# A decoder step on one core: the feed-forward's weight sums move from DRAM to VectorE, gate/up takes both token halves from one weight load, down becomes a stage of its own

## The chip, the core and the metric

The kernel runs on one core of a Trainium2 chip. TensorE (PE) multiplies matrices, VectorE (DVE) and ScalarE (ACT) do elementwise work, GpSimd (POOL) does some too, and SyncE (SP) issues DMAs between DRAM and the on-chip memory SBUF. Each engine works through its own queue in order. Matrix products land in PSUM, eight banks that PE writes and DVE and ACT read. The metric is the device time of one launch in microseconds (us), smaller is better.

## What is computed

One layer of a hybrid decoder for 1024 prompt tokens and 64 sample tokens (1088 columns in all): a combined input projection, sliding-window attention and an mLSTM side by side, an output projection, cross-attention to a memory, and a SwiGLU feed-forward. All of it is float32. The part that the change rewrites is the feed-forward:

```
def swiglu(xn, w_gate, w_up, w_down):
    g = jnp.einsum('btd,df->btf', xn, w_gate)        # D_MODEL 1024 -> FFN_HIDDEN 2816
    u = jnp.einsum('btd,df->btf', xn, w_up)
    return jnp.einsum('btf,fd->btd', jax.nn.silu(g) * u, w_down)
y = y + swiglu(rmsnorm(y, g_ffn), w_gate, w_up, w_down)
y_out = rmsnorm(y, g_final)
```

## The kernel before

Every float32 product is made of three products of halves of the numbers: each operand is split into a rounded part `hi` (an ACT copy to the type fp32r) and the rest `lo` (a DVE subtraction), and `mm3` (L145) adds hi·hi, hi·lo and lo·hi in PSUM. The split of a weight tile is in `prep` (L1111): ACT L1119 and DVE L1120.

The feed-forward uses a seven-product form of the 2x2 block product (Winograd's), with blocks of 128 x 128 weights and 128 x 272 activations. It needs sums and differences of weight blocks and of activation blocks. The 1088 columns are two halves z of 544, each of two blocks of 272. The hidden width is 11 pairs p of 256. A pair of one half takes 14 products in `gate_up` (7 for gate, 7 for up, 12 matmuls each) and 7 in `down` (12 matmuls each).

- The **weight sums** are made before the feed-forward, in DRAM: `make_sums` (L179) issues 36 copies on the ACT queue (L192) into `sgu` and `sdn` and 36 accumulating DMAs on the POOL queue (L187, `accum_op=ALU.add`), one pair of them at each `next(presum)` in the attention part. The feed-forward then loads finished sums.
- The **activation sums** are made in SBUF: of the normed input in `ffn_x` (L1130), of the hidden blocks h in `parts_of` (L1070), with two differences on POOL (L1072, L1073), two more on DVE (L1079, L1080) and splits on ACT and DVE (L1083, L1084).
- The **order**: for each half, `plan` runs gate/up of three pairs, then down of two (L1101), and so on, so that gate/up and down alternate; then the other half. Weights are loaded once for each half, in tiles of 128 x 1024 (512 KB), three raw tiles and three split ones in turn. `down` adds its products from PSUM to y in SBUF on DVE (L1237). At the end `Final` sums squares (L1286, L1287) and writes the normed output (L1300).
- A scheduler orders each engine's queue from its own cost estimates when the kernel is built. A DMA waits in its queue like any instruction.

The attention part (the first 642 us) has, beside PE's work, chains that go through small DMAs: rows of the mLSTM gates are written to DRAM and read back broadcast (`bc` from Md, `wb` from Wd and Wds), masks are loaded (`msk`), y is loaded (L797), weights of the projections (`wraw`, L120).

Of the kernel before, what the change touches and what calls it, by code (L numbers as in the profile page):

```python
# [44 lines left out]
def tile_hymba_step(  # L45
# [118 lines left out]
    sgu = dr.tile([NP2, P, 8, 512], F32, name="sgu")  # L164
    sdn = dr.tile([NP2, P, 4, 512], F32, name="sdn")

    def sums_of(a, b, gu):
        def v(t, i, step):
            t = t[a:b].rearrange("n p e c -> (n p) e c")
            return t[:, i:i + step + 1:step] if gu else t[:, i]  # L170
        if gu:
            R11, R12, R22, R21 = v(wgu, 0, 2), v(wgu, 1, 2), v(wgu, 4, 1), v(wgu, 6, 1)
            s2, s1, s3, s4 = v(sgu, 0, 2), v(sgu, 1, 2), v(sgu, 4, 2), v(sgu, 5, 2)
        else:
            R11, R12, R22, R21 = v(wdn, 0, 1), v(wdn, 1, 1), v(wdn, 2, 1), v(wdn, 3, 1)
            s2, s1, s3, s4 = v(sdn, 0, 1), v(sdn, 1, 1), v(sdn, 2, 1), v(sdn, 3, 1)
        return (s1, R21, R22), (s3, R11, R21), (s2, R11, s1), (s4, R12, s2)

    def make_sums():  # L179

        parts = ([sums_of(a, min(a + 2, NP2), True) for a in range(0, NP2, 2)]
                 + [sums_of(a, min(a + 4, NP2), False) for a in range(0, NP2, 4)])
        copied = []

        def add():
            dst, plus = copied.pop(0)
            tc.keep_in_program_order(G.dma_start(dst, plus, accum_op=ALU.add))  # L187

        for i in range(4):
            for part in parts:  # L190
                dst, src, plus = part[i]
                tc.keep_in_program_order(A.dma_start(dst, src))  # L192
                if len(copied) == 3:
                    add()
                copied.append((dst, plus))
                yield
        while copied:
            add()
            yield
# [107 lines left out]
    for b in range(NB + 1):  # L307
        acc, m = tok_gemm(wb, b, 384)
        r = rt[:m, b:b + 1]
        A.activation(mvx[b // 2][:m, b % 2, 1:4, 0:P],  # L310
                     acc[:m, 0:384].rearrange("p (h e) -> p h e", h=3), AF.Copy, scale=r)
        if b % 3 == 2:
            next(presum)
# [177 lines left out]
    for i, (wi_, pre) in ((1, (2, 0.125)), (2, (3, None)), (3, (4, None))):  # L491
# [9 lines left out]
        next(presum)  # L501
# [123 lines left out]
    for blk in range(NB):  # L625
        if blk == 4:
            mlstm_sample()
            next(presum)
# [23 lines left out]
        next(presum)  # L652
# [383 lines left out]
    sg = slot("r", [4, HC], name="sg")  # L1036

    def ffn_rstd(ci, s_ps):

        mm(s_ps, ones, sg[:, ci])  # L1040
        return rstd_from(rf[:, ci * HC:ci * HC + HC], s_ps, D)

    for ci, (c0, c1) in enumerate(CX):
        ss = sg[:, ci]
        for d in range(NK):
# [24 lines left out]
    def parts_of(out, S):  # L1070

        G.tensor_tensor(S[:, N1], S[:, B11], S[:, B12], ALU.subtract)  # L1072
        G.tensor_tensor(S[:, T3], S[:, B22], S[:, B12], ALU.subtract)  # L1073
        parts(out, S, 4, 7)
        sums_of_blocks(S)
        parts(out, S, 0, 4)

    def sums_of_blocks(S):
        V.scalar_tensor_tensor(S[:, N2], S[:, N1], -1.0, S[:, B22], ALU.mult, ALU.subtract)  # L1079
        V.scalar_tensor_tensor(S[:, T4], S[:, N2], -1.0, S[:, B21], ALU.mult, ALU.subtract)  # L1080

# [12 lines left out]
    def dn_tiles(ps_):
        for src, i in ((wdn, 0), (sdn, 0), (sdn, 2)):
            for p in ps_:
                yield [src[p, :, i:i + 2, :]]
        for i in range(0, len(ps_), 2):
            yield [wdn[p, :, 2:3, :] for p in ps_[i:i + 2]]

    plan = [("gu", 0)]  # L1101
    for g0 in range(0, NP2 - 1, 2):
        plan += [("gu", g0 + 1), ("gu", g0 + 2), ("dn", list(range(g0, g0 + (3 if g0 == 8 else 2))))]

    def tiles_of(plan):
# [3 lines left out]
    todo, ahead = iter([t for _ in range(2) for t in tiles_of(plan)]), []

    def prep():  # L1111
        for srcs in todo:
            raw = fp.tile([P, 2, 512], F32, tag="wr", name="wr", bufs=3)
            i = 0
            for a in srcs:
                nc.sync.dma_start(raw[:, i:i + a.shape[1]], a)
                i += a.shape[1]
# [10 lines left out]
    prep()  # L1128

    def ffn_x(z):  # L1130

        xo, xs = [], []
        for j in range(4):
            S = fp.tile([P, 8, HC], F32, tag="ho" if z == 0 and j > 1 else "hs", name="xs",
                        bufs=3 if z == 0 and j > 1 else 2)
            for i, d in ((B11, j), (B21, j + 4)):
                V.scalar_tensor_tensor(S[:, i:i + 2].rearrange("p a c -> p (a c)"), y[d][:, z * SET:z * SET + SET],  # L1137
                                       gcol(V_FFN, d), rf[:, z * SET:z * SET + SET], ALU.mult, ALU.mult)
            t = fp.tile([P, 2, 7, HC], F32R, tag="xo", name="xo", bufs=4)
            xo.append(t)  # L1140
            if z > 0:
                parts_of(t, S)
                continue
            parts(t, S, 4, 7)
            xs.append(S)
        for S in xs:
            G.tensor_tensor(S[:, N1], S[:, B11], S[:, B12], ALU.subtract)
            G.tensor_tensor(S[:, T3], S[:, B22], S[:, B12], ALU.subtract)
        for S, t in zip(xs, xo):
            sums_of_blocks(S)  # L1150
            parts(t, S, 0, 4)
# [308 lines left out]
```

## Time and profile before

| | |
|---|---|
| time, median of 3 runs (lowest to highest) | 1392.54 us (1391.67 to 1392.87) |
| the profiled execution: its own time, its span | 1396.1 us, 1394.3 us |
| PE matmul busy | 1291.6 us, 93% |
| DVE busy | 938.5 us, 67% |
| ACT busy | 684.2 us, 49% |
| POOL busy | 211.2 us, 15% |
| DMA moved | 244.12 MB |

The span runs from the first to the last instruction. A row of a timeline has its start and duration in us; an idle time of the engine before it stands at the end in brackets, with what ended it ("<-"). `xN` merges N instructions. In a row of stretches, (xN) counts instructions, and PEclk is the TensorE clock granted, 1.00 being the upper of its two levels (2.4 GHz) and 0.50 the lower (1.2 GHz). An instruction of DVE may start before the one ahead of it has ended, so that N of a kind take less than N times their duration.

### The profile page before, as it was taken

To read this page: it belongs to the slowest core of one execution; us is meant where nothing else is said; L and a number is where in the kernel's file an instruction comes from. 1 tells how busy PE (TensorE), PEld (TensorE's weight loads), DVE (VectorE), ACT (ScalarE), POOL (GpSimd) and SP (SyncE) were. 2 spreads that over 40 slices of the span, in tenths; PEclk is the share of its full clock that TensorE was granted. 3 is DMA by queue.
4 is the path that set the end of the run, shared out by engine and by line. 5 is a ranking of instruction groups with operands and counts; after the bars stand their busy time and mean duration, and the time that the engine had idled before them with its cause. 6 is when DMAs were issued, how large, how long until landed. Compare 5 with 4: busy or idle time off the path is not lost.

```text
span 1394.3 us, 23826 instructions
## 1 busy us (share of the span) xinstructions
PE 1291.6 (93%) x9194; PEld 1204.0 (86%) x9194; DVE 938.5 (67%) x1854; ACT 684.2 (49%) x1332; POOL 211.2 (15%) x182
## 2 busy tenths in 40 slices
PE   6999987989989969997999999999998999999996
PEld 6999976877767868765999999999997999999995
DVE  7224333436665656878777878787988868687777
ACT  4332332334755445655654554545567454545463
POOL 2000120220111365314010100001210000101010
PEclk9999988997989999997899999999999999999998
DMA  5167594793999899421555565555455555555543
GB/s 224 38 199 193 156 209 125 198 232 88 243 300 265 232 280 196 137 76 46 162 174 178 156 193 164 180 167 176 154 167 188 180 182 172 177 174 174 175 158 117
DMA packets 96330, 244.12 MB, mean 175 GB/s; under 512 B 10081, under 2 KB 17697, under 8 KB 96217
## 3 DMA queue, kind: packets, MB, share of 16 engines
q1 hardware_dynamic: 61273, 173.40, 39.2%
q0 software_dynamic: 17472, 34.61, 14.7%
q10 hardware_dynamic: 17472, 34.61, 7.3%
q8 instruction: 72, 1.18, 0.3%
q14 instruction: 41, 0.34, 0.1%
HBM read 235.19 MB, written 76.59 MB: 224 GB/s over the span
## 4 chain that ended last, share of the span: by engine, by line
PE 34%; DVE 12%; issue 3%; ACT 3%; POOL 1%; POOLq 0%; DVEq 0%; ACTq 0%
PE b L90 34%; DVE wo L1120 4%; ACT wo L1119 2%; DVE ho L1084 2%; DVE y L1237 1%; POOL h L1072 1%; DVE xo L1084 1%; DVE yo L1300 1%; DVE h L1172 1%; DVE xs L1137 1%; ACT kp L1176 0%; DVE h L1212 0%; DVE h L1204 0%; DVE sg L1201 0%; DVE h L1201 0%
## 5 line engine op out<-in xcount | busy, mean ns | idle before, releaser
L90 PE MATMUL b<-xo,wo 128*128 128x272 f32 x3696 | 476.1, 291 | 17.1 <-ACT wo L1119 7.2
L90 PEld LDWEIGHTS b<-xo,wo 128*128 128x128 f32 x3696 | 470.1, 191 | 22.3 <-ACT wo L1119 8.2
L1120 DVE TENSOR_TENSOR wo<-wr,wo 128x1024 fp32r<-128x1024 f32 x232 | 282.2, 1223 | 104.4 <-ACT wo L1119 104.1
L1119 ACT ACTIVATE wo<-wr 128x1024 fp32r<-128x1024 f32 x232 | 244.0, 1053 | 194.0 <-PE b L90 135.3
L90 PE MATMUL b<-ho,wo 128*128 128x272 f32 x1848 | 237.4, 289 | 5.0 <-DVE wo L1120 2.7
L90 PEld LDWEIGHTS b<-ho,wo 128*128 128x128 f32 x1848 | 233.2, 188 | 8.0 <-DVE wo L1120 4.7
L1072 POOL TENSOR_TENSOR h<-h 128x272 f32<-128x272 f32 x22 | 35.5, 1613 | 587.3 <-DVE h L1172 568.4
L90 PE MATMUL mm<-xhi,whi 128*128 128x384 f32 (+1 forms) x288 | 100.6, 349 | 5.9 <-DVE og L785 5.9
L1237 DVE TENSOR_TENSOR y<-y,b 128x272 f32<-128x272 f32 x280 | 103.0, 429 | 4.3 <-PE b L90 4.1
L90 PE MATMUL mm<-xhi,wlo 128*128 128x384 f32 (+1 forms) x288 | 99.5, 345 | 0.0
L90 PE MATMUL mm<-xlo,whi 128*128 128x384 f32 (+1 forms) x288 | 99.3, 345 | 0.0
L1176 ACT ACTIVATE kp<-b 128x272 f32<-128x272 f32 x132 | 51.5, 394 | 62.9 <-PE b L90 61.9
L108 ACT ACTIVATE whi<-wraw 128x1024 fp32r<-128x1024 f32 x39 | 41.0, 1054 | 70.1 <-PE mm L90 49.8
L90 PE MATMUL mm<-chi,wlo 128*128 128x384 f32 (+1 forms) x192 | 66.6, 348 | 3.7 <-POOL wlo L109 3.6
L90 PE MATMUL mm<-chi,whi 128*128 128x384 f32 (+1 forms) x192 | 67.5, 354 | 2.2 <-ACT whi L108 1.7
L90 PE MATMUL mm<-clo,whi 128*128 128x384 f32 (+1 forms) x192 | 66.4, 346 | 0.0
L90 PEld LDWEIGHTS mm<-xhi,whi 128*128 128x128 f32 x288 | 56.7, 197 | 9.5 <-DVE og L785 6.2
L90 PEld LDWEIGHTS mm<-xlo,whi 128*128 128x128 f32 x288 | 56.6, 197 | 3.1 <-issue 2.0
L90 PEld LDWEIGHTS mm<-xhi,wlo 128*128 128x128 f32 x288 | 56.4, 196 | 3.2 <-issue 1.9
L1084 DVE TENSOR_TENSOR ho<-h,ho 128x816 fp32r<-128x816 f32 (+1 forms) x44 | 48.6, 1141 | 0.0
L1083 ACT ACTIVATE ho<-h 128x816 fp32r<-128x816 f32 (+1 forms) x44 | 42.0, 994 | 11.8 <-DVE h L1212 9.9
L1169 ACT ACTIVATE sg<-sg 128x272 f32<-128x272 f32 x66 | 27.9, 423 | 40.3 <-DVE sg L1201 33.2
(369 smaller groups left out, 1983.9 us busy)
## 6 DMA issues: line engine op xcount, KB each, us to landing
wr<-sgu SPq DMA_DIRECT2D x88, 512.0 KB
wr<-wgu SPq DMA_DIRECT2D x66, 512.0 KB
wr<-sdn SPq DMA_DIRECT2D x44, 512.0 KB
sgu<-wgu ACTq DMA_DIRECT2D x20, 1024.0 KB
wr<-wdn SPq DMA_DIRECT2D x22, 512.0 KB
sgu<-wgu POOLq DMA_DIRECT2D x10, 1024.0 KB, 13.1
sgu<-sgu POOLq DMA_DIRECT2D x10, 1024.0 KB, 20.0
sdn<-wdn ACTq DMA_DIRECT2D x8, 1024.0 KB
```

Of the source, the lines that this page charges most:

```text
L90: return TE.matmul(out, lhsT, rhs, start=start, stop=stop, skip_group_check=skip)
L108: A.activation(hi, src, AF.Copy)
L1072: G.tensor_tensor(S[:, N1], S[:, B11], S[:, B12], ALU.subtract)
L1083: A.activation(out[:, 0, i:j], S[:, i:j], AF.Copy)
L1084: V.tensor_tensor(out[:, 1, i:j], S[:, i:j], out[:, 0, i:j].bitcast(F32), ALU.subtract)
L1119: A.activation(w[:, 0, :i], raw[:, :i], AF.Copy)
L1120: V.tensor_tensor(w[:, 1, :i], raw[:, :i], w[:, 0, :i].bitcast(F32), ALU.subtract)
L1137: V.scalar_tensor_tensor(S[:, i:i + 2].rearrange("p a c -> p (a c)"), y[d][:, z * SET:z * SET + SET], gcol(V_FFN, d), rf[:, z * SET:z * SE ...
L1169: A.activation(sg[:, i], sg[:, i], AF.Silu, scale=scale)
L1172: V.scalar_tensor_tensor(t, t, scale, sg[:, i], ALU.mult, ALU.mult)
L1176: A.activation(t, src, AF.Copy)
L1237: V.tensor_tensor(y[d][:, c0:c0 + HC], y[d][:, c0:c0 + HC], src[dp], op)
```

## The change

It drops `make_sums` with its 72 DMAs and the DRAM tile `sgu`. The feed-forward becomes two stages.

In **gate/up** each weight block (128 x 512, 256 KB) is loaded raw, and `sums` makes the four sums of it in SBUF. For 7 of the 11 pairs both halves z use each split weight tile in turn, so that loads, sums and splits are made once for both; the first two and the last two pairs are done for one half at a time ("single units"), there two of the four sums are on POOL. Of the 15 units, each splits 14 tiles. The results h go to DRAM (`hd`). While a pair is at half 1, `dn_sums` also makes the four sums of its down weights on DVE and stores them (`sdn`). y is put aside in DRAM (`yd`).

**Down** runs after all of gate/up: six groups (4, 4, 3 pairs for each half). h is read back in `h_parts`, which makes all four differences on POOL and splits on ACT and DVE for the next group while a group runs.

```diff
-        for i in range(4):
-            for part in parts:
-                dst, src, plus = part[i]
-                tc.keep_in_program_order(A.dma_start(dst, src))
-                if len(copied) == 3:
-                    add()          # G.dma_start(dst, plus, accum_op=ALU.add)
...
-        next(presum)
...
-    def parts_of(out, S):
-        G.tensor_tensor(S[:, N1], S[:, B11], S[:, B12], ALU.subtract)
-        G.tensor_tensor(S[:, T3], S[:, B22], S[:, B12], ALU.subtract)
...
+    def parts(out, i, src):
+        n = src.shape[1]
+        A.activation(out[:, 0, i:i + n], src, AF.Copy)
+        V.tensor_tensor(out[:, 1, i:i + n], src, out[:, 0, i:i + n].bitcast(F32), ALU.subtract)
+    def diffs(b11, b12, b21, b22, n1, m2, t3, t4, e1=G, e2=G):
+        e1.tensor_tensor(n1, b11, b12, ALU.subtract)
+        e1.tensor_tensor(t3, b22, b12, ALU.subtract)
+        e2.tensor_tensor(m2, n1, b22, ALU.add)
+        e2.tensor_tensor(t4, m2, b21, ALU.subtract)
...
+    def sums(r11, r12, r21, r22, e=V):
+        e.tensor_tensor(s1, r21, r22, ALU.add)
+        V.scalar_tensor_tensor(m2, s1, -1.0, r11, ALU.mult, ALU.subtract)
+        e.tensor_tensor(s3, r11, r21, ALU.add)
+        V.tensor_tensor(s4, r12, m2, ALU.subtract)
...
+            yield from sums(*r, e=V if len(zs) > 1 else G)
...
+    def dn_sums(p):
+        for i, t in enumerate(sums(*[raw(wdn[p, :, i, :]) for i in range(4)])):
+            nc.sync.dma_start(sdn[p, :, i, :], t)
...
+    units = ([(p, (z,)) for z in range(2) for p in (0, 1)] + [(p, (0, 1)) for p in range(2, NP2 - 2)]
+             + [(p, (z,)) for z in range(2) for p in (NP2 - 2, NP2 - 1)])
+    downs = [(z, g) for z in range(2) for g in (range(0, 4), range(4, 8), range(8, NP2))]
...
-            w = fp.tile([P, 2, 2, 512], F32R, tag="wo", name="wo", bufs=3)
-            A.activation(w[:, 0, :i], raw[:, :i], AF.Copy)
-            V.tensor_tensor(w[:, 1, :i], raw[:, :i], w[:, 0, :i].bitcast(F32), ALU.subtract)
+            w = fp.tile([P, 2, 512], F32R, tag="wo", name="wo", bufs=5)
+            A.activation(w[:, 0], t, AF.Copy)
+            V.tensor_tensor(w[:, 1], t, w[:, 0].bitcast(F32), ALU.subtract)
...
+    def x_second(j):
+        norm(a[:, 2:4], j, 1)
+        norm(b[:, 2:4], j + 4, 1)
+        parts(t, B11, a[:, 2:3])
+        parts(t, B21, b[:, 2:4])
+        diffs(a[:, 2], a[:, 3], b[:, 2], b[:, 3], a[:, 0], a[:, 1], b[:, 0], b[:, 1])
+        parts(t, N1, a[:, 0:2])
+        parts(t, T3, b[:, 0:2])
...
+            def product(b, i, start, then):
+                w = next_w()
+                for z in zs:
+                    for j in range(4):
+                        mm3(b[z], w[:, 0, j * P:j * P + P], w[:, 1, j * P:j * P + P],
+                            xo[z][j][:, 0, i], xo[z][j][:, 1, i], start and j == 0, j == 3, True)
+                    then(z, b[z])
...
+        for z in zs:
+            nc.sync.dma_start(hd[z, p], S[z])
+    def h_parts(z, p, tag):
+        hb, hn = slot(tag, [4, HC], name="hb"), slot(tag, [4, HC], name="hn")
+        nc.sync.dma_start(hb, hd[z, p])
+        t = big("ho")
+        parts(t, B21, hb[:, 0:3])
+        diffs(hb[:, 2], hb[:, 3], hb[:, 0], hb[:, 1], hn[:, 0], hn[:, 1], hn[:, 2], hn[:, 3])
+        parts(t, N1, hn)
...
+    xo[0] = x_first()
+    for u, (p, zs) in enumerate(units):
+        gate_up(u, p, zs)
+        if u < 2:
+            xo[1] += [x_second(2 * u), x_second(2 * u + 1)]
+    load_yy(0, "z")
+    hs = [h_parts(0, p, "m") for p in downs[0][1]]
...
+    for i, (z, g) in enumerate(downs):
+        if i == 3:
+            load_yy(1, "m")
+        nz, ng = downs[i + 1] if i + 1 < len(downs) else (0, ())
+        hs = down(z, hs, [(nz, p, "m" if i < 3 else "z") for p in ng],
+                  (lambda d, cc: fin[0].add(d, cc, False)) if i == 2 else fin[1].add if i == 5 else None,
+                  first_final if i == 3 else None)
```

In the attention part POOL's queue loses its DMAs. Before, around the sample tokens of the mLSTM (QZ, bcs) and the block behind them (bc, wb):

```order
L187 DMA sdn<-wdn 512x512
L587 MEMSET QZ 128x1088
L187 DMA sdn<-wdn 512x512
L553 TENSOR_TENSOR bcs<-c,bcs 64x256
L553 TENSOR_TENSOR bc<-c,bc 128x512
L637 TENSOR_TENSOR wb<-mqk,wb 128x128 x2
L187 DMA sdn<-wdn 384x512
```

The same place in the changed kernel:

```order
L593 TENSOR_TENSOR wb<-mqk,wb 128x128 x2
L544 MEMSET QZ 128x1088
L510 TENSOR_TENSOR bcs<-c,bcs 64x256
L510 TENSOR_TENSOR bc<-c,bc 128x512
L593 TENSOR_TENSOR wb<-mqk,wb 128x128 x2
```

The DMAs of line 187 are gone, the rest keeps its order.

On DVE, where a gate/up ends and a down of two pairs begins before (wo is a split weight tile, ho a split of h, y<-y,b the adding of a product):

```order
L1120 TENSOR_TENSOR wo<-wr,wo 128x1024
L1079 SCALAR_TENSOR_TENSOR h<-h 128x272
L1212 SCALAR_TENSOR_TENSOR h<-b,sg 128x272
L1080 SCALAR_TENSOR_TENSOR h<-h 128x272
L1120 TENSOR_TENSOR wo<-wr,wo 128x1024
L1084 TENSOR_TENSOR ho<-h,ho 128x816
L1084 TENSOR_TENSOR ho<-h,ho 128x1088
L1237 TENSOR_TENSOR y<-y,b 128x272 x8
L1120 TENSOR_TENSOR wo<-wr,wo 128x1024 x2
```

And in the changed kernel, in its down stage, in the second group (hb is the h read back, hn POOL's four differences of it):

```order
L1036 TENSOR_TENSOR ho<-hb,ho 128x816
L1036 TENSOR_TENSOR ho<-hn,ho 128x1088
L1227 TENSOR_TENSOR yy<-yy,b 128x272 x4
L1095 TENSOR_TENSOR wo<-wr,wo 128x512 x3
L1036 TENSOR_TENSOR ho<-hb,ho 128x816
L1095 TENSOR_TENSOR wo<-wr,wo 128x512
L1036 TENSOR_TENSOR ho<-hn,ho 128x1088
L1227 TENSOR_TENSOR yy<-yy,b 128x272 x4
L1095 TENSOR_TENSOR wo<-wr,wo 128x512 x4
```

The two differences that DVE made (lines 1079, 1080) are POOL's now, and each stretch of four additions has one pair's splits of h beside it, where these stood between gate/up units before.

## Rows read from the trace of the kernel before

**Rows 1.** Stretches: busy us (xcount) of PE, PEld, DVE, ACT, POOL; PEclk, DMA, GB/s.

```profile
642.00:666.50 24.50, 12.60 (x45) 9.29 (x43) 24.17 (x31) 13.62 (x19) 10.56 (x9) 0.59 0.20 65
1000.00:1100.00 100.00, 92.04 (x694) 89.06 (x694) 86.89 (x141) 65.12 (x97) 11.68 (x11) 0.98 0.55 173
1200.00:1300.00 100.00, 99.33 (x792) 98.89 (x791) 80.24 (x126) 51.53 (x70) 7.27 (x6) 1.00 0.55 172
```

**Rows 2.** Timeline of PE, attention part, rows after a long idle time.

```profile
194.17 0.80 PE L90 MATMUL pt<-mvx,S 128*128 128x129 f32 x2 [5.52 <-DVE S L562]
231.18 3.67 PE L90 MATMUL pt<-CS,QZ 128*64 128x129 f32 x16 [7.00 <-DVE QZ L593]
315.10 0.63 PE L90 MATMUL mm<-xhi,whi 128*128 128x320 f32 x1 [5.89 <-DVE og L785]
414.05 0.42 PE L90 MATMUL sc<-khi,qhl 64*128 64x256 f32 x2 [3.61 <-DVE qhl L109]
436.61 1.14 PE L769 MATMUL pt<-c,sp 128*128 128x128 f32 x8 [3.33 <-DVE sp L679]
493.97 0.44 PE L90 MATMUL mm<-chi,wlo 128*128 128x384 f32 x1 [1.79 <-POOL wlo L109]
522.47 1.68 PE L90 MATMUL sc<-kvhl,qhl 64*128 64x256 f32 x12 [5.58 <-ACT qhl L108]
```

**Rows 3.** Timeline of POOL, DVE and ACT ahead of five of these.

```profile
191.33 1.26 POOL L553 TENSOR_TENSOR bc<-c,bc 128x512 f32<-128x512 f32 x1 [15.86 <-DMA bc<-Md]
230.65 1.64 DVE L593 TENSOR_TENSOR QZ<-mqk,wb 64x32 f32<-64x32 f32 x8 [8.01 <-DMA wb<-Wds]
310.82 0.36 DVE L709 CUSTOM_DVE_ANT_0 spS<-sc,msk 128x192 f32<-128x192 f32 x1 [7.86 <-DMA msk<-cst_sw]
413.24 0.56 DVE L864 TENSOR_TENSOR y<-y,mm 128x384 f32<-128x384 f32 x1 [3.75 <-DMA y<-xT]
517.60 1.06 ACT L108 ACTIVATE whi<-wraw 128x1024 fp32r<-128x1024 f32 x1 [5.80 <-DMA wraw<-wout]
```

**Rows 4.** Queues from 350 to 440 us: packets, MB, share of the 16 DMA engines.

```profile
q0 software_dynamic: 4484, 8.90, 57.5%
q10 hardware_dynamic: 5001, 9.90, 31.7%
```

**Rows 5.** Stretches of the attention part.

```profile
150.00:350.00 200.00, 179.01 (x1114) 150.67 (x1113) 88.19 (x285) 70.65 (x244) 36.19 (x40) 0.91 0.72 174
350.00:450.00 100.00, 90.19 (x587) 71.03 (x585) 60.54 (x235) 59.63 (x191) 13.24 (x11) 0.95 1.08 272
450.00:560.00 110.00, 93.71 (x547) 85.25 (x545) 67.28 (x119) 52.08 (x114) 54.02 (x35) 0.95 0.94 231
```

**Rows 6.** Timeline of DVE in the feed-forward.

```profile
796.04 2.86 DVE L1237 TENSOR_TENSOR y<-y,b 128x272 f32<-128x272 f32 x8
798.82 2.35 DVE L1120 TENSOR_TENSOR wo<-wr,wo 128x1024 fp32r<-128x1024 f32 x2
```

**Rows 7.** Groups by form on DVE: busy us, mean ns | idle before, releasers.

```profile
L1120 DVE TENSOR_TENSOR wo<-wr,wo 128x1024 fp32r<-128x1024 f32 x230 | 280.9, 1227 | 104.4 <-ACT wo L1119 104.1
L1300 DVE SCALAR_TENSOR_TENSOR yo<-y,vv,rf 128x272 f32<-128x272 f32 x32 | 13.6, 495 | 4.3 <-ACT rf L161 4.3
```

**Rows 8.** Timeline: POOL and DVE at the same time, twice.

```profile
639.62 2.48 POOL L1052 TENSOR_TENSOR sg<-sg,sq 128x272 f32<-128x272 f32 x3 [3.53 <-ACT sq L1051]
640.58 0.44 DVE L1009 TENSOR_TENSOR y<-y,mm 128x272 f32<-128x272 f32 x1 [0.30 <-PE mm L90]
...
518.73 2.35 POOL L109 TENSOR_TENSOR wlo<-wraw,whi 128x1024 fp32r<-128x1024 f32 x1 [5.16 <-ACT whi L108]
519.66 1.83 DVE L115 SCALAR_TENSOR_TENSOR nhl<-y,vv,nhl 128x384 fp32r<-128x384 f32 x1 [6.96 <-ACT nhl L114]
521.88 0.60 DVE L115 SCALAR_TENSOR_TENSOR nhl<-y,vv,nhl 128x384 fp32r<-128x384 f32 x1
```

**Rows 9.** Timeline of POOL: a difference of 512 columns.

```profile
156.16 1.30 POOL L553 TENSOR_TENSOR bc<-c,bc 128x512 f32<-128x512 f32 x1 [32.42 <-DMA bc<-Md]
```

More of the change, by code (lines that the diff above doesn't have):

```diff
@@ L1109, in tile_hymba_step, with big @@
[L1109 to L1120 removed]
+    def big(name):
+        return fp.tile([P, 2, 7, HC], F32R, tag="big", name=name, bufs=8)
@@ new lines, in tile_hymba_step, with all_ops @@
+    downs = [(z, g) for z in range(2) for g in (range(0, 4), range(4, 8), range(8, NP2))]
+    def all_ops():
+        for p, zs in units:
+            yield from gu_ops(p, zs)
+            if zs[-1] == 1:
+                dn_sums(p)
+        for z, g in downs:
+            yield from dn_ops(g)
+    todo, ahead = all_ops(), []
+    def prep():
+        for t in todo:
+            w = fp.tile([P, 2, 512], F32R, tag="wo", name="wo", bufs=5)
+            A.activation(w[:, 0], t, AF.Copy)
+            V.tensor_tensor(w[:, 1], t, w[:, 0].bitcast(F32), ALU.subtract)
@@ L1206, in gate_up @@
[L1206 to L1219 removed]
+            product(b1, T3, False, result(H22, "p5", -1.0))
@@ new lines, in gate_up @@
+            product(b3, B22, False, result(H12, "p16"))
+            product(b1, T4, False, last)
+        for z in zs:
[7 more added lines that the diff above has]
+        parts(t, N1, hn)
+        return t
@@ L1220, in down, with second, product @@
+    yy = [[None] * 4, [None] * 4]
+    def down(z, hs, ahead_of, done=None, after_first=None):
+        n, nxt, ahead_of = len(hs), [], iter(ahead_of)
         b1 = [bank(i) for i in (1, 2, 6, 7)]
-        b2 = [bank(i) for i in (4, 5, 0, 3)]
-        b3 = [None] * 4
-        def prod(b, ws, o, i, start, e):
+        def second():
+            return [bank(i) for i in (4, 5, 0, 3)]
+        def product(b, i, start, dd, cc, op=ALU.add, last=False, also=None):
             for q in range(n):
-                w, o_ = ws(q, o)
+                w = next_w()
@@ new lines, in product @@
+                        V.tensor_tensor(v, v, b[dp], op)
+                        if last and done:
+                            done(2 * dp + dd, cc)
+            for a in ahead_of:
+                nxt.append(h_parts(*a))
+                break
+        product(b1, B11, True, 0, 0)
+        if after_first:
+            after_first()
+        product(second(), B21, True, 0, 0, last=True)
+        product(b1, M2, False, 0, 1)
+        b3 = second()
+        product(b3, N1, True, 1, 1, ALU.subtract)
@@ L1272, in tile_hymba_step @@
+        product(b1, T3, False, 1, 1, ALU.subtract, last=True)
+        product(b3, B22, False, 0, 1, last=True)
+        product(b1, T4, False, 1, 0, ALU.subtract, last=True)
+        return nxt
     class Final:
@@ L1306, in tile_hymba_step @@
[L1306 to L1322 removed]
+            if self.n[cc] == NK and now:
+                self.out(cc, bank((2, 0)[cc]))
@@ new lines, in tile_hymba_step, with first_final @@
+    fin = [Final(0), Final(1)]
+    def first_final():
+        for cc in range(2):
+            fin[0].out(cc, bank((3, 0)[cc]))
+    for i, (z, g) in enumerate(downs):
[5 more added lines that the diff above has]
+                  first_final if i == 3 else None)
```

313 lines of the change are left out of this document (103 added, 210 removed).

## The prediction

> **What bounds the kernel now.** I read first how full each stretch of the feed-forward is. From 1200 to 1300 us PE is busy 99.33 of 100 us at the full clock, 792 matmuls at 0.1254 us each [rows 1]: that pace is the floor there, and the change leaves the number of matmuls (5544 in the feed-forward) and their shape alone. PE falls short of it in three places. From 642 to 666.5 us the normed input is made and DVE is busy 24.17 of 24.5 us; from 1000 to 1100 us the second half's input is made and the first half's output written, and only 694 matmuls run; and there is a short tail. In the steady stretch DVE has a fifth of its time left. Next I read PE's timeline in the attention part for long idle times, and who released them. Seven rows [rows 2] show 5.52, 7.00, 5.89, 3.61, 3.33, 1.79 (the first of three like it) and 5.58 us, some 36 us in all. Going back from each to the engine ahead of it, I find a DMA: bc from Md, wb from Wds, the masks, y from xT, projection weights [rows 3]. The DMA engines are full there: from 350 to 440 us the accumulating queue q0 and the copying queue q10 alone, which carry only the weight sums, take 57.5% and 31.7% of all sixteen [rows 4]. PE also runs part of this time at the lower clock after such gaps: mean granted 0.91, 0.95 and 0.95 over 200, 100 and 110 us [rows 5], or 18 + 5 + 5.5 = 28.5 us of work lost.
>
> **Part 1, the 72 DMAs go.** At best all 36 us of idle time and 24 of the 28.5 us of clock come back (-60). At worst nothing does, because each wait names only what came last, and a softmax or mLSTM step on DVE and ACT may be ready barely earlier (0). The small loads (a 64-row broadcast that kept DVE idle 8.01 us, masks 7.86 us [rows 3]) should lose most of their time with 89% of the traffic gone, so I take two thirds of the idle time, 24 us, and 13 us of the clock: **-37**. Next late are then the in-order chains of ACT and DVE.
>
> **Part 2, the second half's input no longer cuts the feed-forward in the middle.** The stretch from 1000 us lacks (792 - 694) x 0.1254 = 12 us against the steady one [rows 1]: **-12**. Its work returns in parts 3 and 4, counted there.
>
> **What DVE's new work costs.** Instructions behind one another overlap a little. Eight additions of 272 columns take 2.86 us and one 0.44 [rows 6, 8], so each takes (2.86 - 0.44) / 7 = 0.346 us. Two splits of 1024 take 2.35 us and one 1.23 [rows 6, 7], so 1.12. On the line through both, 512 columns take 0.59, 544 take 0.63, 816 take 0.91, 1088 take 1.19. The output multiplication, 0.495 alone [rows 7], takes 0.40 in a row. On POOL a difference of 272 takes 2.48 / 3 = 0.83 [rows 8], one of 512 takes 1.30 [rows 9].
>
> A unit of both halves has 14 splits, 8 sums of gate/up and 4 of down (26 x 0.59) and 20 evacuations of 272 (6.9): 22 us of DVE beside 336 x 0.1254 = 42 us of PE, and no POOL. All of that is hidden, against 80% of DVE before; I count 0 for the seven units.
>
> POOL and DVE are not independent. Beside three POOL sums an addition that reads y and PSUM still takes 0.44 us, but a DVE instruction with its operands in SBUF, 0.60 alone, takes 1.83 and ends with the POOL split that runs from 518.73 to 521.08 [rows 8]. So POOL's time can be added to DVE's when DVE works on SBUF operands. I call s the share of POOL's time that DVE loses. It lies between 0 and 1. In the stage of part 4 the instructions on SBUF alone are 141 of 223 us (185 less 39 of additions and 5 of evacuations from PSUM), 0.63; I take 0.6.
>
> **Part 3, the first four single units.** Until the fourth has ended DVE's queue has 16 normings of 544 (10.0 us), the splits of the input (17.3), 8 differences (2.8), 58 weight splits (34.4), 27 sums (16.0) and 40 evacuations (13.8), 94.3 us. PE needs 4 x 168 x 0.1254 = 84.3 us and starts in earnest 22 us after DVE [rows 1], as before: 106.3. POOL adds the differences of the second half's input, 16 x 0.83, and 16 sums, 16 x 1.30, 34.1 us. DVE's excess is 94.3 + 34.1 s - 106.3: at s = 0.6 **+8**, at most +22, at least 0.
>
> **Part 4, from the last two single units to the fourth group of down.** Here 131 splits (77.7), 14 sums (8.3), 20 evacuations (6.9), 20 times the two splits of h (41.8), 112 additions to y (38.8), 14 sums of squares (4.8) and 16 output multiplications (6.4) make 184.7 us on DVE. PE needs 2 x 168 + 15 x 84 matmuls: 200.1 us; five split tiles ahead, 12 matmuls each, are 7.5 us more. POOL has 8 sums (10.4) and 80 differences (66.4): 76.8 us, where before a pair had two short ones. Excess 184.7 + 76.8 s - 207.6: at s = 0.6 **+23**, from 0 to +54. Reading h back costs no more than that: 7 x 256 KB and 544 KB a pair in 84 x 0.1254 = 10.5 us are 227 GB/s, which at the 0.55 share for 172 GB/s [rows 1] fills 0.73 of the DMA engines. A wait that this adds: DVE stands at the split of hn until POOL's four differences are done, with the weight splits behind it, and PE waits for those once its five tiles are used up.
>
> **Part 5, shorter distances.** In a single unit a bank is evacuated within one product of 12 matmuls, 1.5 us. Most of the 112 evacuations (0.44 us) fit; about a third may stand behind a split and cost 0.1: **+4** (0 to 12).
>
> **Sum.** -37 - 12 + 8 + 23 + 4 = -14 on the profiled execution's 1396.1 us, 1382; the runs' median, 1392.5, lies 3.6 below that execution, so 1379. In s the sum is 111 s - 80, zero at s = 0.72.
>
> The Trainium skill ("SBUF — State Buffer", who interferes with whom) says that the port that GpSimd shares with VectorE is an exclusive lock when the VectorE instruction has two SBUF inputs, and that an instruction with one does not contend. Both rows above agree. It gives no share s; taken at its hardest, with no POOL time beside additions, the sum would be that of s = 1, which is the end of rival A.
>
> **Rivals.**
>
> - A, POOL holds DVE and DVE sets the pace of down: s from 0.72 up. For it: the four differences stand behind one another in POOL's queue, in the same stretches as the splits of h and the weight splits, and DVE is in order and cannot bring its additions forward. Against it: 39 us of additions and any idle time of DVE are free for POOL. At s = 0.9 the sum is +20: 1412; at s = 1, +31: 1424. Slower. Chance 0.27.
> - B, the attention part hardly gains, because the softmax chains are late anyway. For it: before 436.61 and 414.05 PE waits on DVE itself [rows 2]. Against it: DVE's own wait ahead of that is for y's DMA, 3.75 us [rows 3]. With -8 in place of -37: +15, 1407. Chance 0.12.
> - C, nearly all of the waits and clock come back (-55) and POOL falls beside the additions and idle time (s = 0.3, parts 3 and 4 at 0): -55 - 12 + 4 = -63, 1330. Chance 0.15.
> - That the weights are still read twice for four pairs is so by the code, but changes no sum: loads are not late there now.
>
> **How the numbers follow.** The forecast, 1379, has 0.46, with 1360 to 1392 as its own range, some of it no change. A measurement of this kernel tells about 0.2% (2.8 us) from no change. Faster: the larger part of the forecast (0.40) and C (0.15), 0.55. Same: 0.08, from the edge of the forecast, A and B. Slower: the rest of A and B, 0.37. The range for 8 in 10 takes half of C and all of A but its end: 1342 to 1422.
>
> **What would show it.** In the attention part the idle rows before QZ (7.00), og (5.89) and S (5.52) shrink below 2 us and PE reaches the feed-forward near 605 us in place of 642. In the double units PE is busy 99% with DVE near 55%. In down, splits of 512 columns show a mean near 0.8 to 1 us in place of 0.69 (on the line from 0.44 to 1.23), and PE waits for wo; the matmuls of a group of three take more than 31.5 us. I am wrong if PE is 99% busy through down (C), if it stands at 85% or less there (A), or if it still waits for the DMA-fed chains before 600 us (B).

## The result and the profile after

The changed kernel takes 1404.18 us (median of 4 runs, 1403.87 to 1407.81) beside 1392.11 us (4 runs) of the kernel before: 1.0099 times the time, interval 1.0073 to 1.0124. It is slower by 12 us where 13 us faster were forecast. Its profiled execution takes 1407.81 us, its span is 1406.0 us.

The attention part gained more than forecast and the feed-forward lost more than that. The feed-forward's first product starts at 592.32 us in place of 650.33. The answer to [rows 5] in the changed kernel, the same stretches of the attention part (time, PE busy, PEld, DVE, ACT, POOL, then PE's clock, DMA share and GB/s):

```profile
150.00:350.00 200.00, 196.20 (x1283) 163.03 (x1282) 106.03 (x366) 88.41 (x305) 19.64 (x27) 0.97 0.24 71
350.00:450.00 100.00, 97.52 (x651) 84.16 (x650) 67.99 (x213) 58.92 (x176) 12.72 (x7) 1.00 0.23 77
450.00:560.00 110.00, 101.36 (x688) 85.56 (x687) 82.18 (x170) 67.59 (x164) 43.83 (x33) 1.00 0.35 111
```

PE is busy 98, 98 and 92% of the three at a mean granted clock of 0.97 to 1.00, and the DMA share is a quarter to a third. The longest of what it still waits for from 150 to 582 us (us in total, times, longest) are instructions of DVE; QZ and og of [rows 2] are no longer in this list and S is down from 5.52 to 1.9:

```profile
PE pt L904 <- DVE sp L898: 4.8, 6, 1.7
PE pt L724 <- DVE sp L634: 2.4, 3, 1.9
PE pt L90 <- DVE S L519: 1.9, 1, 1.9
```

In the stretch of [rows 4], the queues q0 and q10 (57.5% and 31.7% there) are gone and the rest stands at

```profile
q1 hardware_dynamic: 2304, 6.55, 21.2%
```

The feed-forward in the changed kernel, from its first product, cut near its stages: input and first four half units (the single units of the change); the double units and the first of the last four half units; the next two; the last and the first groups of down; the end.

```profile
592.30:743.00 150.70, 116.47 (x808) 111.10 (x809) 128.59 (x187) 73.93 (x141) 49.67 (x37) 0.87 0.41 131
743.00:1040.00 297.00, 297.00 (x2370) 297.00 (x2369) 181.49 (x329) 115.23 (x245) 8.27 (x6) 1.00 0.40 128
1040.00:1079.00 39.00, 38.33 (x307) 38.11 (x305) 33.27 (x54) 21.95 (x45) 9.78 (x6) 1.00 0.44 149
1079.00:1323.00 244.00, 210.56 (x1527) 205.00 (x1528) 216.25 (x336) 124.52 (x201) 102.71 (x90) 0.94 0.68 215
1323.00:1406.00 83.00, 69.90 (x547) 68.69 (x546) 62.40 (x130) 34.92 (x63) 1.67 (x3) 0.93 0.48 149
```

The same lengths from the first product of the kernel before:

```profile
650.30:801.00 150.70, 144.15 (x1086) 141.49 (x1087) 120.68 (x172) 84.30 (x115) 17.65 (x15) 0.93 0.51 158
801.00:1098.00 297.00, 287.41 (x2246) 283.36 (x2246) 244.53 (x381) 167.97 (x237) 31.06 (x26) 0.99 0.57 175
1098.00:1137.00 39.00, 38.63 (x309) 38.41 (x308) 30.43 (x52) 17.41 (x25) 2.42 (x2) 1.00 0.56 175
1137.00:1381.00 244.00, 241.16 (x1915) 239.76 (x1913) 190.97 (x303) 127.47 (x181) 17.06 (x14) 1.00 0.53 164
1381.00:1394.30 13.30, 1.28 (x2) 0.50 (x2) 7.58 (x19) 1.78 (x4) 0.00 (x0) 0.60 0.50 168
```

Read the matmul counts, not the busy time, which holds stalled and slow matmuls too. A double stretch runs 2370 in 297 us, 0.1253 us each; the time that a stretch takes beyond count x 0.1253 is its loss.

| loss, us | before | after | difference |
|---|---|---|---|
| input and first half units (150.7 us) | 14.6 | 49.5 | +34.9 |
| the next 297 us | 15.6 | 0.0 | -15.6 |
| the next 39 us | 0.3 | 0.5 | +0.2 |
| last half units, down (244 us) | 4.1 | 52.7 | +48.6 |
| the rest | 13.0 | 14.5 | +1.5 |

That is +69.6 us, and with -58.0 ahead of the first product +11.6, which is the difference of the spans (1406.0 - 1394.3 = 11.7). The double units do what was forecast: PE without a gap, DVE busy 181.49 of 297 us (61%). The losses sit at both ends, where POOL works. In 40 us pieces of the changed kernel around down:

```profile
1080.00:1120.00 40.00, 30.95 (x211) 30.30 (x210) 29.37 (x39) 17.16 (x33) 18.67 (x16) 0.87 0.61 194
1120.00:1160.00 40.00, 31.83 (x220) 30.30 (x219) 38.03 (x50) 22.46 (x31) 27.95 (x24) 0.91 0.68 217
1160.00:1200.00 40.00, 37.75 (x295) 36.83 (x294) 37.16 (x53) 21.80 (x33) 18.63 (x16) 1.00 0.67 211
1200.00:1240.00 40.00, 38.01 (x290) 37.73 (x290) 33.99 (x62) 20.79 (x34) 8.09 (x8) 0.96 0.66 207
1240.00:1280.00 40.00, 38.00 (x295) 37.17 (x294) 37.54 (x83) 19.47 (x39) 0.89 (x2) 1.00 0.77 241
1280.00:1320.00 40.00, 30.01 (x196) 28.68 (x195) 36.59 (x48) 21.21 (x30) 25.93 (x23) 0.87 0.66 215
```

The first two and the last lose 13.6, 12.4 and 15.4 us, 41.4 of the 52.7. The second and the last have the most POOL time, and the first has the last half units. In the second down begins, while inputs of its first and second groups are made; the last lies inside the fourth group, while those of the fifth are made. The pieces between lose 3.0, 3.7 and 3.0, the first of them with 18.63 us of POOL, so POOL's time by itself doesn't tell the loss. DVE's busy time doesn't either: 37.54 of 40 us from 1240 go with a loss of 3.0, and 29.37 of 40 us from 1080 with 13.6.

### The profile page after: what moved, and what is told of

Its sections match the earlier page's. It is cut to its first block, busy times and chain, and to the rows that moved or that the text cites. A ratio compares the mean times of both kernels' runs of the same rounds, so it can differ in the third digit from the quotient of the medians.

```text
span 1406.0 us, 24487 instructions
## 1 busy us (share of the span) xinstructions
PE 1290.0 (92%) x9194; PEld 1203.2 (86%) x9194; DVE 963.1 (68%) x1962; ACT 653.0 (46%) x1466; POOL 268.8 (19%) x230
## 5 line engine op out<-in xcount | busy, mean ns | idle before, releaser
L90 PE MATMUL b<-xo,wo 128*128 128x272 f32 x3696 | 483.8, 293 | 48.1 <-DVE h L1168 14.4
L90 PE MATMUL b<-ho,wo 128*128 128x272 f32 x1848 | 246.5, 295 | 24.4 <-DVE wo L1095 14.3
L90 PEld LDWEIGHTS b<-ho,wo 128*128 128x128 f32 x1848 | 241.2, 194 | 29.3 <-DVE wo L1095 17.1
L1095 DVE TENSOR_TENSOR wo<-wr,wo 128x512 fp32r<-128x512 f32 x244 | 182.7, 776 | 76.9 <-ACT wo L1094 76.7
L1094 ACT ACTIVATE wo<-wr 128x512 fp32r<-128x512 f32 x244 | 150.6, 626 | 114.6 <-PE b L90 80.5
L1094 ACT ACTIVATE wo<-ws 128x512 fp32r<-128x512 f32 x120 | 74.1, 627 | 94.7 <-PE b L90 66.4
L1095 DVE TENSOR_TENSOR wo<-ws,wo 128x512 fp32r<-128x512 f32 x120 | 90.9, 766 | 30.3 <-ACT wo L1094 29.9
L1054 POOL TENSOR_TENSOR ws<-wr 128x512 f32<-128x512 f32 x16 | 24.5, 1530 | 385.1 <-DMA sdn<-ws 303.1
L1227 DVE TENSOR_TENSOR yy<-yy,b 128x272 f32<-128x272 f32 x168 | 64.0, 433 | 6.3 <-PE b L90 6.0
L109 POOL TENSOR_TENSOR wlo<-wraw,whi 128x1024 fp32r<-128x1024 f32 x12 | 28.9, 2406 | 173.8 <-ACT whi L108 172.8
```

The lines of the kernel that those rows point to most:

```text
L90: return TE.matmul(out, lhsT, rhs, start=start, stop=stop, skip_group_check=skip)
L109: (eng or V).tensor_tensor(lo, src, hi.bitcast(F32), ALU.subtract)
L1054: e.tensor_tensor(s1, r21, r22, ALU.add)
L1094: A.activation(w[:, 0], t, AF.Copy)
L1095: V.tensor_tensor(w[:, 1], t, w[:, 0].bitcast(F32), ALU.subtract)
L1227: V.tensor_tensor(v, v, b[dp], op)
```

## The experiments

Times are medians; a ratio is to the kernel before, run on the same chip, with its 95% interval. Differences in us are to the 1404.18 of the changed kernel, which these runs did not have beside them, so that a few us more or less say nothing. Three theories are named in the expectations: L (POOL holds DVE), Q (loads come late from SyncE's queue) and A (one split weight tile ahead is too few).

**The transfers alone (before_nosums).**

```diff
-    presum = make_sums()
+    presum = iter(int, 1)
-        for src, i in ((wgu, 0), (wgu, 2), (sgu, 0), (sgu, 2), (sgu, 4), (sgu, 6), (wgu, 4)):
+        for src, i in ((wgu, 0), (wgu, 2), (wgu, 0), (wgu, 2), (wgu, 4), (wgu, 6), (wgu, 4)):
```

(and wdn in place of sdn.)

> The kernel before without the 72 transfers that make block sums in DRAM; its feed-forward reads unsummed weights in their place (the sums are left out, the number and size of its loads stay). This is the first step of the prediction by itself, put there at -37 us. If the transfers alone held the attention part, the feed-forward's first product starts near 592 as in the changed kernel and the time is 1331 to 1340 (-52 to -60). If half of the 58 us came from what else changed around it (queues, buffers, the y copies), it is 1350 to 1365.

1341.03 us, 0.963 (0.9588 to 0.9673): 50 us less than the kernel before beside it (1391.20), 1 us above the range for the transfers alone. Its attention part is nearly the changed kernel's, 415.95 us of PE busy in 150 to 582 us and 414.76 there, and its first product of the feed-forward starts at 596.71 us: 53.6 of the 58.0 us go with the 72 transfers alone, and 4.4 with something else of the change.

**The differences of down left out (nodiff).**

```diff
-        diffs(hb[:, 2], hb[:, 3], hb[:, 0], hb[:, 1], hn[:, 0], hn[:, 1], hn[:, 2], hn[:, 3])
-        parts(t, N1, hn)
+        parts(t, N1, hb)
```

> Leaves out the 88 differences of the down stage on GpSimd: the blocks themselves are split in their place, so the down sums are of other data and the tiles hn are gone. Against 1404 of the changed kernel. Theory L (GpSimd holds VectorE, and VectorE bounds the stretch 1079 to 1323, which lost 53 us of TensorE time): most of that loss goes, 1369 to 1380, and the 512-wide splits there fall back to 0.69 us. Theory Q (the raw loads stand in one queue on SyncE with six buffers, and hb comes back late from DRAM): under 10 us go, 1394 to 1402. Theory A (one operand ahead is too little when a product takes 1.5 us): under 10 us go as well.

1376.56 us, 0.9903 (0.9866 to 0.994): 27.6 us go, and the loss from 1079 to 1323 falls from 52.7 to 22.1 us. That is in theory L's range; but three things went at once: POOL's hold on DVE, ACT's wait for hn, and the tiles hn.

**The hold without the wait (hold_only), without wait and tiles (hold_noslot), the tiles without the hold (slots).**

```diff
 hold_only:
-        parts(t, N1, hn)
+        parts(t, N1, hb)
 hold_noslot, besides:
-        hb, hn = slot(tag, [4, HC], name="hb"), slot(tag, [4, HC], name="hn")
+        hb = slot(tag, [4, HC], name="hb")      # differences go to one scratch tile
 slots, in place of diffs:
+        G.memset(hn[:, 0, 0:8], 0.0)
+        G.tensor_tensor(hn[:, 0, 0:8], hn[:, 0, 0:8], hb[:, 0, 0:8], ALU.add)
+        parts(t, N1, hb)
```

> GpSimd makes the 88 differences of down as in the changed kernel, but the splits behind them read the blocks in their place, so that no engine waits for GpSimd there (the differences are left out of the result). It parts the two ways in which GpSimd can cost: holding VectorE's port (the 512-wide splits took 793 ns beside it and 685 without it, 1257 against 1001 and 1449 against 1284 for the two wider ones: some 28 us of VectorE in all) and being waited for (ScalarE stood 36.1 us at hn in its order, with the weight splits behind). If the hold is the cost: 1394 to 1404, as changed. If the wait is: 1376 to 1384, as in the run without the differences. If each has a part: 1385 to 1393.

> Four 272-wide differences per unit on GpSimd as in the changed kernel, but into one scratch tile that nobody reads; the splits read the blocks (the differences are left out of the result), and the 22 tiles hn are not allocated, so that hb has the four buffers for itself. It is hold_only without the buffers' part: GpSimd beside VectorE and nothing else. If the hold on VectorE is the whole 27.6 us: 1398 to 1406. If it is the buffers (hn and hb share four): 1376 to 1384. Between them if both.

> The run without the differences, with the tiles hn allocated again and touched by two 8-wide GpSimd instructions each (the splits read the blocks, so the differences are left out of the result). The buffers' part without the hold. If the hold is the whole cost: 1375 to 1382, as without the tiles. If the buffers are: 1396 to 1406.

hold_only: 1404.43 us, 1.0094 (1.0056 to 1.0131). hold_noslot: 1404.59, 1.008 (1.0052 to 1.0108). slots: 1380.37, 0.9898 (0.9871 to 0.9925). The first is 0.4 us past its range for the hold, the other two are inside theirs. hold_only doesn't settle it alone: no engine waits for the differences there, but SyncE's queue waits 58.2 us for POOL to be done with hb before it can load the next. hold_noslot does: in it nothing waits for the differences for more than 0.5 us in all, and the time is still that of the changed kernel; with the tiles but next to no POOL work (slots) it is that of nodiff. In the changed kernel ACT stood at hn for 36.1 us (16 times),

```profile
ACT ho L1035 <- POOL hn L1042: 36.1, 16, 3.5
```

and with this wait gone and the hold left the time did not fall.

The hold shows in DVE's durations. The changed kernel from 1079 us on, groups of DVE (line, names, shapes, count, busy us, mean ns, idle before):

```profile
L1095 DVE TENSOR_TENSOR wo<-wr,wo 128x512 fp32r<-128x512 f32 x161 | 121.4, 793 | 21.4 <-ACT wo L1094 21.3
L1227 DVE TENSOR_TENSOR yy<-yy,b 128x272 f32<-128x272 f32 x168 | 64.0, 433 | 6.3 <-PE b L90 6.0
L1036 DVE TENSOR_TENSOR ho<-hn,ho 128x1088 fp32r<-128x1088 f32 x22 | 31.9, 1449 | 4.3 <-ACT ho L1035 4.3
L1036 DVE TENSOR_TENSOR ho<-hb,ho 128x816 fp32r<-128x816 f32 x22 | 27.7, 1257 | 2.0 <-ACT ho L1035 1.9
```

and the run slots:

```profile
L1095 DVE TENSOR_TENSOR wo<-wr,wo 128x512 fp32r<-128x512 f32 x160 | 104.1, 685 | 22.1 <-ACT wo L1094 21.9
L1228 DVE TENSOR_TENSOR yy<-yy,b 128x272 f32<-128x272 f32 x168 | 64.3, 433 | 12.8 <-PE b L90 12.5
L1036 DVE TENSOR_TENSOR ho<-hb,ho 128x1088 fp32r<-128x1088 f32 x22 | 28.3, 1285 | 0.0
L1036 DVE TENSOR_TENSOR ho<-hb,ho 128x816 fp32r<-128x816 f32 x22 | 22.0, 1002 | 2.7 <-ACT ho L1035 2.5
```

and hold_noslot, the splits of weights and of the four blocks:

```profile
L1095 DVE TENSOR_TENSOR wo<-wr,wo 128x512 fp32r<-128x512 f32 x161 | 125.3, 817 | 13.7 <-ACT wo L1094 13.6
L1036 DVE TENSOR_TENSOR ho<-hb,ho 128x1088 fp32r<-128x1088 f32 x22 | 31.6, 1435 | 0.0
```

The splits, which read and write SBUF alone, are longer by 17, 4 and 6 us in all in the changed kernel than in slots; the additions to yy, with one operand in PSUM, are at 433 ns in both. That is some 27 us of DVE for 101.0 us of POOL (the four lines of differences, 27.8, 25.1, 24.3 and 23.8 us).

**The differences on DVE (diffs_dve).** `diffs(..., V, V)` in `h_parts`.

> The 88 differences of the down stage run on VectorE, all else as changed. By the undisturbed 272-wide rows they are some 0.37 us each there, 33 us of VectorE work in 280 us. Theory L: VectorE loses more to a held port than it does by the work, 1384 to 1398. Theory Q or A: VectorE only gets more work, 1404 to 1416.

1397.03 us, 1.0034 (1.0008 to 1.0061): 7 us go, inside L's range at its near end. DVE has 38 us of differences (88 x 0.434 us, which overlap a little) in place of 27 us of hold and the time still falls; why is open.

**The sums of the half units on DVE (sums_dve), the down sums in the double units (dn_early).**

```diff
 sums_dve:
-            yield from sums(*r, e=V if len(zs) > 1 else G)
+            yield from sums(*r, e=V)
 dn_early, in all_ops:
-            if zs[-1] == 1:
-                dn_sums(p)
+            if len(zs) > 1:
+                dn_sums(p)           # and those of pairs 0, 1, 9, 10 amid units 2 to 5
```

> The 32 sums that GpSimd makes in the eight half units run on VectorE, all else as changed. Theory L (GpSimd holds VectorE in the half units too): 4 to 12 us go, 1392 to 1400, most of it from 642 to 743 and 1079 to 1123. Rival (GpSimd is hidden there and VectorE is simply full): 1404 to 1412.

> The block sums of the down weights are all made in the seven double units (where VectorE is 58% busy and TensorE 100%) and none in the four half units that follow or end the gate and up stage. Theory Q (sums for down put four raw loads and VectorE waits into the half units): 10 to 18 us go, 1386 to 1394, from 698 to 743 and 1079 to 1123. Theory L: the work of four sums, 4 x 4 x 0.6 us of VectorE, goes, and less than 8 us of time, 1396 to 1404.

sums_dve: 1392.63 us, 1.0018 (0.9988 to 1.0048), -11.5. dn_early: 1390.64 us, 1.0014 (0.9984 to 1.0045), -13.5. Each makes up the difference to the kernel before within its interval; sums_dve is in L's range. In the input and first half units the loss falls from 49.5 to 42.7 and to 40.3 us. The last 44.6 us of these in the changed kernel and, without a gap, in dn_early:

```profile
698.40:743.00 44.60, 37.71 (x278) 37.27 (x278) 29.06 (x50) 17.43 (x37) 2.52 (x2) 0.92 0.47 148
698.40:743.00 44.60, 44.60 (x357) 44.60 (x357) 31.58 (x55) 21.51 (x46) 1.75 (x1) 1.00 0.56 174
```

dn_early's number is what theory Q said. It takes 16 sums away from DVE too, but DVE was busy only 29.06 of these 44.6 us, so its work had not run out of time there; from 642 to 745 us POOL stands 24.4 us (4 times) for raw loads ahead of its sums, and ACT 14.9 us (4 times) for sums. That points to the loads, though Q's other test (gq, below, of the loads of hb and yy) failed: the loads' part is not shown by a run of its own.

**Two operands ahead (look2).** `prep()` called once more before the loop.

> Two split weight operands ahead of TensorE in place of one (one more call before the loop; five buffers as before). Theory A: the split of the next operand no longer stands behind the evacuation of the product before, and 20 to 40 us go, 1364 to 1384. Theories L and Q: the engines' work is the same and only single stalls are covered, 1396 to 1404.

1403.98 us, 1.0112 (1.0054 to 1.0169). Theory A falls: a second operand in hand brought nothing.

**The queue that loads hb and yy (gq).** `nc.gpsimd.dma_start` for both.

> The down stage's loads of hb and yy are issued from GpSimd's queue in place of SyncE's, all else as changed. In the changed kernel the chain of waits stands at hb four times, 3.15 to 5.96 us, 17.6 us in all. Theory Q (they come late because SyncE's queue issues in order behind raw loads that wait for buffers): 8 to 18 us go, 1386 to 1396. Theory L (they are late only because everything is late; and their issue now stands behind GpSimd's differences): 1398 to 1408.

1432.52 us, 1.026 (1.0195 to 1.0325): slower by 28, which neither theory had. POOL's work where the first inputs are made:

```profile
1132.21 1.52 POOL L1041 TENSOR_TENSOR hn<-hn,hb 128x272 f32<-128x272 f32 x1
1133.68 0.57 POOL L1202 DMA_DIRECT2D hb<-hd  x1
1134.27 0.78 POOL L1042 TENSOR_TENSOR hn<-hn,hb 128x272 f32<-128x272 f32 x1
1137.97 0.77 POOL L1039 TENSOR_TENSOR hn<-hb 128x272 f32<-128x272 f32 x1 [2.92 <-DMA hb<-hd]
```

Each load is issued only behind differences of the pair before, and POOL then stands until it lands: load and differences take turns, 7 to 10 us a pair from 1104 to 1182 us, where in the changed kernel the pairs from 1123 to 1138 us follow one another in 4.5 to 5.6.

**No half units at the end (double_end).** `range(2, NP2)` in the list of double units.

> The last two weight units are run for both token halves from one load too; no half units at the end. The 56 splits and 32 sums of two half units go, and the first down group's four inputs can only be made when the products end. If the half units' own work is what costs there: 5 to 15 us go, 1389 to 1399. If the cover that they give to the first down group's inputs is worth more than that: TensorE stands 15 to 25 us ahead of down, 1405 to 1415.

1401.33 us, 1.0068 (1.0043 to 1.0092): between the two, -3 us. What leaving out the half units saves there and what their cover for the first inputs of down is worth nearly cancel; the run doesn't part them.

**Several at once (early, gq_dve, best2, best_sp).** early is dn_early with the differences made by DVE at the end of each gate/up unit (those of pairs 0 and 1 in units 2 and 3) and stored beside h:

```diff
+    def h_new(z, p, h):
+        hn = slot("z", [4, HC], name="hn")
+        diffs(h[:, 2], h[:, 3], h[:, 0], h[:, 1], hn[:, 0], hn[:, 1], hn[:, 2], hn[:, 3], V, V)
+        nc.sync.dma_start(hd[z, p, :, 4:8], hn)
```

best2 and best_sp also make the half units' weight sums once, in the first pass or amid double units, and read them back:

```diff
+    def gu_again(p):
+            for i in range(4):
+                yield raw(sgu[KEPT[p], :, 4 * m + i, :])
```

> The down weights' sums as in the run that made them all in the double units, and the 88 differences of the feed-forward activations made on VectorE in the gate and up stage, kept in DRAM beside them (twice the bytes of hd), so that down has neither GpSimd work nor differences. Theory L with Q's part added: the 27.6 us of leaving the differences out and the 13.5 us of the early sums come together, 1360 to 1368, which is 2% below both kernels. If they overlap (both free VectorE between 1079 and 1200): 1368 to 1378.

> Four single edits together: the down weights' sums in the double units (-13.5 alone), the sums of the half units on VectorE (-11.5 alone), the down differences on VectorE (-7 alone), hb and yy loaded from GpSimd's queue. If they add up: 1364 to 1373. If they free the same stretch, and VectorE is then full by its own work from 1123 to 1323 (it was busy 190 of 200 us with the differences): 1376 to 1386.

> The run with differences and down sums made early, with two more edits: hb, hn and yy are loaded from GpSimd's queue, and the sums of the four half units' weights are made once (by VectorE, in the first pass or in double units) and kept in DRAM, so that GpSimd makes no sums and the second pass none at all. If SyncE's order held the inputs of down (9.5 us ahead of the first group, 8.7 ahead of the fourth in that run): 1352 to 1366, faster than both kernels. If the bytes hold them (DMA share 0.93 in that stretch): 1372 to 1384.

> The run best2 with hb, hn and yy loaded from SyncE's queue again, as in the changed kernel: differences, down sums and the half units' sums made early or once. The move to GpSimd's queue alone cost 28 us where that engine made differences; here it makes next to none. If SyncE's order holds the inputs of down more than GpSimd's does: 1380 to 1388. If GpSimd's queue was no help: 1370 to 1378.

early: 1385.74 us, 0.9949 (0.9917 to 0.9982). gq_dve: 1388.69, 0.9973 (0.994 to 1.0005). best2: 1378.54, 0.9908 (0.9881 to 0.9935). best_sp: 1379.24, 0.9903 (0.9869 to 0.9936). The gains don't add up: early should have had up to 41 us and has 18, which misses both its ranges, and gq_dve missed both of its own. early's own trace shows the new limit: PE stands 9.48 us in down's first group and 8.73 us in the fourth,

```profile
1117.44 21.42 PE L90 MATMUL b<-ho,wo 128*128 128x272 f32 x144 [9.48 <-ACT wo L1102]
...
1265.82 22.20 PE L90 MATMUL b<-ho,wo 128*128 128x272 f32 x156 [8.73 <-ACT wo L1102]
```

because ACT, in order, stands at hn's load (22.8 us in all, 10.8 at once), where the DMA share is 0.93:

```profile
1079.00:1123.00 44.00, 31.42 (x221) 30.09 (x220) 31.70 (x49) 25.10 (x40) 0.81 (x1) 0.85 0.93 315
```

The chain that ended last runs, ahead of the first of these, through the store of hn (5.34 us) and a load of hn (6.55 us), and ahead of the second through the output of the first half (4.61 us) and a load of hn (7.28 us). DVE's hold became a wait for DMAs. best2 and best_sp differ by less than their intervals, so with POOL nearly free the queue that issues these loads made no difference. best2 came out in the range for bytes, best_sp between its two. Both beat the kernel before by 1%, and so the changed kernel by nearly 2% (0.9908 / 1.0099 = 0.981).

## Why the prediction was wrong

**Part 1, the transfers: right in mechanism, too small.** Forecast -37, measured -58.0 in the trace, of which before_nosums shows 53.6 (50 in time); the bound was -60. From 150 us to 10 us ahead of the first product PE is idle 17.2 us in place of 53.1 (-35.9, where 24 was taken of 36) and busy 414.76 in place of 436.92 with nearly as many matmuls, 2757 and 2780 (-22.2, where 13 was taken of 28.5). I had held back a third of the waits for chains on DVE and ACT that would be late next; they were not.

**Part 2, the cut in the middle: right.** Forecast -12, measured -15.6. The double units cost nothing, as forecast.

**Parts 3 and 4, the steps that failed.** Forecast +8 and +23 (and +4 of part 5), measured +34.9 and +48.6. Of the marks that were named, the splits came out at 793 ns, just under the 0.8 to 1 us of the forecast, and PE was busy 86% from 1079 to 1323 us by the row, just above A's mark, and 78% by its matmuls. The share s was not the fault: 27 us of DVE for 88 differences that part 4 priced at 0.83 us, 73 us, is s = 0.37, less than the 0.6 taken, and part 4's formula with it gives 184.7 + 76.8 x 0.37 - 207.6 = +5.5. What failed is the step "Excess 184.7 + 76.8 s - 207.6": it sets the sum of DVE's work against PE's time over the whole stage, as if DVE's 23 us of free time could take in every hold and nothing but DVE's work could keep PE waiting.

Neither held. The hold was paid nearly us for us, 24 to 28 us of time for 27 us of DVE, though DVE was idle 11% of the 244 us. That this is close to the 23 forecast for part 4 is luck: a smaller share without the free time. And at s = 0 the formula has no excess at all (184.7 against 207.6), but nodiff, without POOL's differences, still loses 22.1 us there, 18 more than the kernel before. The 22.1 us stand where the last half units and the first inputs meet (8.3 and 6.4 us lost) and inside the fourth group (6.9 us):

```profile
1080.00:1120.00 40.00, 34.34 (x253) 33.33 (x253) 33.09 (x50) 25.02 (x42) 5.25 (x4) 0.96 0.77 259
1120.00:1160.00 40.00, 35.34 (x268) 34.91 (x268) 32.34 (x58) 20.50 (x31) 0.00 (x0) 0.96 0.75 245
1200.00:1240.00 40.00, 40.00 (x322) 40.00 (x321) 38.60 (x79) 26.85 (x49) 0.00 (x0) 1.00 0.64 202
1240.00:1280.00 40.00, 34.97 (x264) 33.43 (x263) 36.92 (x70) 21.45 (x34) 0.00 (x0) 1.00 0.93 300
```

It is not a full DVE: it is busy 33 and 32 of 40 us in the first two, and the third, with 38.60, loses nothing. The chain that ended last in nodiff runs there through loads of weights:

```profile
1117.33 6.19 DMA wr<-wdn
1134.12 6.16 DMA wr<-sdn
```

and in the fourth group through the output of the first half. hb of the fifth group takes the buffers of yy, so its loads are issued only after the 16 output multiplications and the stores behind them, and ACT stands at hb with the weight splits behind it:

```profile
1244.34 6.70 DVE L1270 SCALAR_TENSOR_TENSOR yy<-yy,vv,rf 128x272 f32<-128x272 f32 x16
1245.28 6.30 SPq L1271 DMA_DIRECT2D o_y<-yy  x8
1253.49 1.85 SPq L1202 DMA_DIRECT2D hb<-hd  x3
1257.72 5.43 ACT L1035 ACTIVATE ho<-hb 128x816 fp32r<-128x816 f32 x6 [3.19 <-DMA hb<-hd]
```

The prediction had put these waits at nothing ("Reading h back costs no more than that", "loads are not late there now"). The bytes came out as forecast, 0.68 of the DMA engines for 0.73, the waits for single loads did not. They are read from the chain; no run takes them away by themselves.

Part 3 failed in the same step. DVE is busy 99.5 of the first 106.1 us, where 39 us are lost, and only 29.06 of the last 44.6, which lost 9.8. Sums and down sums taken off the half units gave 7 and 9 us of loss back; how the rest divides between DVE's work, POOL's hold and waits for loads stays open. Some of it comes from the making of the input, which I had counted alike for both. The kernel before, whose split tile carries two operands, runs 34 matmuls in the waits of its first 16 us; the changed kernel runs 14 in 21 us and then waits for a weight once more:

```profile
603.94 0.59 PE L90 MATMUL b<-xo,wo 128*128 128x272 f32 x1 [1.29 <-ACT xo L1035]
606.63 0.82 PE L90 MATMUL b<-xo,wo 128*128 128x272 f32 x2 [2.10 <-DVE xo L1036]
613.10 9.22 PE L90 MATMUL b<-xo,wo 128*128 128x272 f32 x58 [5.65 <-DVE wo L1095]
```

This is read from the timelines; no run tries it by itself.

**The rivals.** The time is near rival A's (1412) by a sum of other terms: POOL does hold DVE, but at s = 0.37, far below A's 0.72, and the hold is 24 to 28 of the 83.5 us that parts 3 and 4 cost. Rival C was right about the attention part and B wrong.

For the hold itself, the Trainium skill ("SBUF — State Buffer", who interferes with whom) says that a VectorE instruction with two SBUF inputs contends with a GpSimd instruction that reads SBUF, and that one with at most one SBUF input, outside the two-port modes, does not. The rows agree: 433 and 433 ns for the additions from PSUM, 793 and 685 for the splits. Of POOL's 101 us beside DVE 27 were lost to it.

## What to carry to other kernels

A sum of work set against a sum of time over a whole stage is a lower bound only; look at the pieces in which the work falls due, and follow what each waits for there. How busy an engine is in a piece is not enough to call it the limit: 38.60 of 40 us of DVE went with no loss in nodiff, and 29.37 of 40 with 13.6 us of loss in the changed kernel. When work moves to another engine, find out by leaving it out, and by keeping it with nobody waiting, whether it costs by what it holds or by who waits for it, the next load of its input included. Transfers in the background are not free: price them by the waits and the clock of the part that they run beside.

## What the runs showed of the hardware that was not expected

- 72 accumulating and copying transfers beside the attention part cost the kernel before 50 us. Of the 58.0 us that the trace of the changed kernel gains there, some 22 are PE's busy time for nearly as many matmuls (mean granted clock 0.94 before and 0.99 after, from 150 us to 10 us ahead of the first product).
- POOL and DVE slow each other. A 272-wide difference of down takes POOL 0.77 us in its shortest rows and 1.15 us on the mean of 88; the 512-wide split takes DVE 793 ns on the mean with the differences in the stage and 685 without. In the rows below a split of 1088 columns, 1.28 us in slots, begins while one difference runs and takes 1.64, and the next difference, at 1.70, begins while the split runs:

```profile
1117.24 0.77 POOL L1041 TENSOR_TENSOR hn<-hn,hb 128x272 f32<-128x272 f32 x1
1118.09 1.70 POOL L1042 TENSOR_TENSOR hn<-hn,hb 128x272 f32<-128x272 f32 x1
1117.52 1.64 DVE L1036 TENSOR_TENSOR ho<-hn,ho 128x1088 fp32r<-128x1088 f32 x1
```

- The same difference takes 434 ns on DVE. On POOL it took 2.6 times as long and cost DVE 0.31 us (27 / 88) all the same.
